# Both MLPs keep their results over the blocks; half of one more block by seven products; adaLN sums and tile pool rearranged

## The chip, the cores and the metric

The kernel runs on one core of a Trainium2 chip. The metric is the device time of one execution in microseconds (us). A run of the kernel before is given as the median of three executions.

## The reference

Two layers over x of 256 tokens by 2048. Each layer does, with a conditioning vector c,

```
mod = silu(c) @ w_ada[l] + b_ada[l]          # 2048 x 12288: six vectors of 2048
sh_a, sc_a, g_a, sh_m, sc_m, g_m = split(mod)
h = rmsnorm(x) * (1 + sc_a) + sh_a
mix = concat(diff_attention(h @ w_in ...), latent_attention(...)) @ w_o[l]
x = x + g_a * mix
h = rmsnorm(x) * (1 + sc_m) + sh_m
y = square(relu(h @ w_mlp_in[l])) @ w_mlp_out[l]     # 2048 -> 8192 -> 2048
x = x + g_m * y
```

and the end is a last rmsnorm with a weight. All numbers are float32.

## The kernel before

Every weight passes the core once, in pieces of 1 MB (128 x 2048), loaded by SyncE's queue (SP) into a pool of five buffers, `raw`. The tensor engine (PE) multiplies in a rounded 32-bit format; to keep float32 accuracy each weight piece is split: ScalarE (ACT) rounds it to `hi` (L154) and VectorE (DVE) takes the rest, `lo` (L157), each in two halves of 128x1024. A product is then three matmuls: hi with both parts of x, lo with the large part (L314, L315, L317).

The adaLN vectors `mod` come from 192 further loads of 1 MB (`ada`), in the same five buffers; on each, DVE does one multiplication with a running sum over 128x2048 (L383). Which place of the program gets how many of them is set by a rate: each piece of weights adds `self.rate` to a credit, and one `ada` is loaded for each whole credit (`more_ada`). Its sum on DVE is issued at the next piece, behind that piece's last split.

x stays on the chip as two halves of 128 tokens (half 0 and half 1), in four chunks c of 512 columns. A result of an output projection (w_o, w_mlp_out) comes chunk by chunk, in four pieces of weights kq each (`rows`), and `updates` does yg = result * gate (L1320), x += yg (L1322), for both halves; where it is the last addition before a norm, ACT squares x besides (L1336). In the last chunk before a norm half 0 is finished before half 1, so that the norm can begin.

An MLP runs in four blocks fb of 2048 hidden columns. For each block the first matmuls (`wides`, L220 and L223) give `hid`; then the rows of w_mlp_out for this block are applied. Columns 0 to 1023 (chunks 0 and 1) can be done "by seven": for a pair of hidden tiles the 2x2 product of blocks is formed with seven products in place of eight (`seven`, L1202 to L1204), which asks DVE for sums of weight blocks (`comb`), more splits, and sums of hid (`sl`, `sh`); at the end `four` adds the seven results up to four tiles (L1238 to L1251). Layer 1 does all its blocks by seven; layer 0 does half of the hidden tiles of block 3 by seven (the other half by `both_by_k`, L1172 to L1178) and blocks 0 to 2 plainly. At the end of each block `updates` adds gate * result to x; in layer 0 block 0's results wait for block 1, since the gate vector is not there yet.

The Tile framework's scheduler sets each engine's order of instructions from priorities and dependences; the order given here is what it wrote.

Of the kernel before, what the change touches and what calls it, by code (L numbers as in the profile page):

```python
# [19 lines left out]
NK = D // P  # L20
# [4 lines left out]
NFB = DFF // D  # L25
# [70 lines left out]


RATE_A0, RATE_V, RATE_K, RATE_M = 1.1, 1.6, 0.6, 0.75
RATE_P = 1.0
RATE_K1, RATE_A1, RATE_C1, RATE_A2, RATE_V1, RATE_O1 = 0.0, 0.8, 0.3, 0.4, 1.2, 0.8  # L100
FILL = "0|1|2|3||||rlm"


class Trunk:
    def __init__(self, ctx, tc, io):
        self.nc, self.tc, self.io = tc.nc, tc, io
        pool = lambda name, bufs, **k: ctx.enter_context(tc.tile_pool(name=name, bufs=bufs, **k))
        self.cp = pool("cp", 1)
        self.wp = pool("wp", 4)
        self.up = pool("up", 40)  # L110
        self.tp = pool("tp", 6)
        self.sp = pool("sp", 8)
        self.pp = pool("pp", 8, space=bass.MemoryType.PSUM)
        self.dp = pool("dp", 1, space=bass.MemoryType.DRAM)
        self.ada_todo, self.ada_here, self.rate, self.credit = [], [], 0.0, 0.0
        self.sums, self.by_act, self.by_dve = [], [], []
        self.bias_out = None
        self.quiet = False
        self.tot = None
        self.n = 0  # L120
# [18 lines left out]
    def weights(self, src, width=2048, order=None):  # L139
        raw = self.raw(src, width)  # L140
        half = width // 2
        out = []
        for i in range(2):
            w, ins = self.part(raw, i, half, order and order[1], order and order[0])
            out.append(w)
        self.more_ada(ins)
        return out

# [739 lines left out]
    def layer(self, l, acc=None):  # L888
        nc, io = self.nc, self.io
# [32 lines left out]
        kk, qn, kn, qr, vm, a, at, v, o = [], [], [], [], [], [], [], [], []  # L922
# [134 lines left out]
        o = self.mo + o  # L1057
        for kq in (2, 3):
            self.rows_by_k(pss, self.weights(io["w_o"][l, 0, kq]), o, kq)
        self.updates(pss, 0, True)  # L1060
        for c in range(1, 4):
            self.updates(self.rows(io["w_o"][l], o, c, c == 3), c, True)

        self.quiet = False
        self.rate = RATE_K1 if l else RATE_K
        h, banks = self.norm_then_by_k(l, 3, 4, io["w_m0"] if l == 0 else io["w_m01"])
        self.rate = RATE_M
        if l:
            for fb in range(NFB):
                self.block_by_seven(1, fb, fb, h, banks, len(banks))  # L1070
                banks = []
        else:
            self.mlp(h, banks)
        self.quiet = False

    def mlp(self, h, banks):

        io = self.io
        late = []
        for fb in range(NFB - 1):  # L1080
# [8 lines left out]
            if fb == 1:  # L1089
                self.gate(0, 5)  # L1090
            for c in range(4):
                pss = self.rows(io["w_m2"][0, fb], hid, c)
                if fb == 0:
                    late += [self.copy(ps, "y") for ps in pss]
                else:
                    if late:
                        pss = [self.added(late.pop(0), ps) for ps in pss]
                    self.updates(pss, c)
        self.block_by_seven(0, NFB - 1, NFB, h, [], NK // 2)

    def block_by_seven(self, l, fb, b, h, banks, plain):

        io = self.io
        hid, steps, sums = [], [], []
        first = NK * fb - (6 if l else 12)
        if l == 0:
            self.rate = RATE_P
# [18 lines left out]
        if l == 0:  # L1126
            self.rate = RATE_M
        elif fb == 0:
            self.gate(1, 5)
        end = fb == NFB - 1  # L1130
        if end and l == 0:
            done = lambda pss, c: self.updates(pss, c, True)
        else:
            done = self.final if end else self.updates
        first, adds, halves = self.four(sums)
        first()
        light = adds + [lambda c=c: done(halves[c], c) for c in range(2)]
        pss = [self.bank("pr") for _ in range(2)]
        for kq in range(4):
            self.rows_by_k(pss, self.weights(io["w_m2"][l, fb, 2, kq]), hid, kq)  # L1140
            if kq < 3 or not plain:
                light.pop(0)()
        done(pss, 2)
        if plain:
            self.both_by_k(b, plain // 2, hid, halves)
            light.pop(0)()
        if end:
            light.pop(0)()
            pss = self.rows(io["w_m2"][l, fb], hid, 3, True)
        else:  # L1150
            pss = [self.bank("pr") for _ in range(2)]
            for kq in range(4):
                self.rows_by_k(pss, self.weights(io["w_m2"][l, fb, 3, kq]), hid, kq)
                if light:
                    light.pop(0)()
        done(pss, 3)

    def both_by_k(self, b, n, xs, halves):

# [68 lines left out]

        return [five, two]

    def four(self, sums):

        add = self.nc.vector.tensor_tensor
        p1, p2, p3, p4, p5, p6, p7 = sums
        c11, c12, c21, c22 = [self.t("y") for _ in range(4)]

        def first():
            self.nc.scalar.activation(c11, p1, AF.Copy)  # L1238
# [384 lines left out]
def _layout(i):  # L1623
# [21 lines left out]
    for l in range(2):  # L1645
# [26 lines left out]
    blocks = [(1, b) for b in range(NFB)] + [(0, NFB - 1)]  # L1672
# [22 lines left out]
```

## Time and profile before

| | us |
|---|---|
| median of 3 runs | 2147.52 (2147.2 to 2147.98) |
| the profiled execution | 2146.1 |
| its span, first to last instruction | 2144.3 |
| mean granted clock of PE | 0.996 |
| PE busy | 2116.9 (99%) |
| DVE busy | 1810.8 (84%) |
| ACT busy | 1212.5 (57%) |

Matmuls overlap: a row's duration of 0.39 us for a 128x512 matmul holds its way through the engine, and the next one starts 0.23 us later. Two starts, not a duration, tell what one costs. The same holds in small on DVE and ACT. In a timeline "[0.96 <-ACT hi L154]" is the idle time of the engine ahead of that instruction and what ended it.

### The profile page before, as it was taken

What the parts mean: (1) busy time and instruction counts of PE and PEld (TensorE: products, weight loads), DVE (VectorE), ACT (ScalarE), POOL (GpSimd) and SP (SyncE); (2) the same over time, 40 slices, a digit from 0 to 9 for tenths busy, and PEclk for the clock granted to TensorE, in tenths of its full rate; (3) what the DMA queues carried; (4) which work ended last, traced back from release to release, by engine and by line L of the source; (5) the groups of instructions that cost most, each with busy time, mean ns of one, the idle gap of its engine ahead of it and who ended that gap; (6) DMA issues with size and microseconds to landing.
All of it is one profiled execution on the core that took longest, in us unless ns stands there. A gap on an engine that the chain in (4) does not pass through costs nothing.

```text
span 2144.3 us, 29298 instructions
## 1 busy us (share of the span) xinstructions
PE 2116.9 (99%) x11239; PEld 1829.4 (85%) x11239; DVE 1810.8 (84%) x2505; ACT 1212.5 (57%) x1847; POOL 6.2 (0%) x18
## 2 busy tenths in 40 slices
PE   7999999999999999999999999999999999999998
PEld 6899887898888888888888898888888888888886
DVE  8889888988788988889987887778977887897897
ACT  6555663565465355346555576547645765664674
POOL 0000000000000000000000000000000000000000
PEclk8999999999999999999999999999999999999999
DMA  9989898799888888886877767875565574564553
GB/s 397 423 343 339 323 355 346 286 332 361 320 326 348 332 337 324 347 330 252 299 253 290 278 224 287 292 267 192 181 237 183 179 247 146 204 230 175 193 191 128
DMA packets 87244, 594.75 MB, mean 277 GB/s; under 512 B 9856, under 2 KB 10304, under 8 KB 20288
## 3 DMA queue, kind: packets, MB, share of 16 engines
q1 hardware_dynamic: 85536, 586.41, 73.7%
q0 software_dynamic: 848, 5.28, 0.6%
q8 instruction: 88, 1.44, 0.3%
q10 hardware_dynamic: 720, 1.19, 0.1%
q14 instruction: 52, 0.43, 0.1%
HBM read 589.66 MB, written 3.18 MB: 276 GB/s over the span
## 4 chain that ended last, share of the span: by engine, by line
PE 93%; DVE 3%; DMA 2%; ACT 2%; issue 1%; ACTq 0%; DVEq 0%; SPq 0%
PE ps L220 20%; PE ps L223 10%; PE pr L314 10%; PE pr L315 10%; PE pr L317 10%; PE pk L263 3%; PE pk L287 3%; PE pp L1203 2%; PE pp L1202 2%; PE pp L1204 2%; PE pv L301 2%; PE pv L299 2%; PE pv L300 2%; PE pk L197 1%; PE pk L201 1%; PE pk L284 1%
## 5 line engine op out<-in xcount | busy, mean ns | idle before, releaser
L154 ACT ACTIVATE hi<-raw 128x1024 fp32r<-128x1024 f32 (+2 forms) x714 | 713.6, 1015 | 549.0 <-PE pr L315 163.9
L157 DVE TENSOR_TENSOR lo<-raw,hi 128x1024 fp32r<-128x1024 f32 (+2 forms) x714 | 821.1, 1170 | 209.6 <-ACT hi L154 98.8
L220 PE MATMUL ps<-h,hi 128*128 128x512 f32 x1952 | 461.9, 390 | 0.0
L383 DVE SCALAR_TENSOR_TENSOR ada<-ada,cond 128x2048 f32<-128x2048 f32 x192 | 438.5, 2286 | 13.3 <-DMA ada<-in_w_ada 12.8
L220 PEld LDWEIGHTS ps<-h,hi 128*128 128x128 f32 x1952 | 362.3, 188 | 74.7 <-DVE sum L1401 1.9
L314 PE MATMUL pr<-hi,hid 128*128 128x512 f32 x704 | 274.0, 389 | 0.0
L315 PE MATMUL pr<-hi,hid 128*128 128x512 f32 x704 | 273.9, 389 | 0.0
L223 PEld LDWEIGHTS ps<-h,lo 128*128 128x128 f32 x1952 | 247.7, 191 | 8.0
L223 PE MATMUL ps<-h,lo 128*128 128x256 f32 x1952 | 250.3, 283 | 0.0
L317 PE MATMUL pr<-lo,hid 128*128 128x512 f32 x704 | 174.5, 389 | 0.0
L317 PEld LDWEIGHTS pr<-lo,hid 128*128 128x128 f32 x704 | 132.2, 188 | 27.4
L315 PEld LDWEIGHTS pr<-hi,hid 128*128 128x128 f32 x704 | 132.2, 188 | 27.4
L314 PEld LDWEIGHTS pr<-hi,hid 128*128 128x128 f32 x704 | 132.2, 188 | 27.3
L1400 ACT ACTIVATE sum<-ps 128x256 f32<-128x256 f32 x110 | 42.0, 382 | 130.5 <-PE ps L223 130.2
L157 DVE TENSOR_TENSOR lo<-comb,hi 128x1024 fp32r<-128x1024 f32 x66 | 80.2, 1221 | 6.3 <-PE ps L223 6.2
L263 PE MATMUL pk<-hf,w 128*128 128x256 f32 x384 | 83.9, 379 | 0.0
L263 PEld LDWEIGHTS pk<-hf,w 128*128 128x128 f32 x384 | 72.7, 190 | 10.0
L154 ACT ACTIVATE hi<-comb 128x1024 fp32r<-128x1024 f32 x66 | 69.2, 1053 | 11.4 <-PE pp L1204 7.6
L197 PE MATMUL pk<-h,hi 128*128 128x256 f32 x256 | 72.3, 285 | 0.2 <-ACT h L718 0.2
L201 PE MATMUL pk<-h,lo 128*128 128x256 f32 x256 | 72.4, 283 | 0.0
L200 PE MATMUL pk<-h,hi 128*128 128x256 f32 x256 | 72.4, 283 | 0.0
L287 PE MATMUL pk<-h,hi 128*128 128x512 f32 x256 | 67.6, 394 | 0.0
(294 smaller groups left out, 3134.4 us busy)
## 6 DMA issues: line engine op xcount, KB each, us to landing
raw<-in_w_m SPq DMA_DIRECT2D x198, 1024.0 KB, 5.6
ada<-in_w_ada SPq DMA_DIRECT2D x192, 1024.0 KB, 6.4
raw<-in_w_ms SPq DMA_DIRECT2D x40, 1024.0 KB, 5.1
raw<-in_w_o SPq DMA_DIRECT2D x32, 1024.0 KB, 5.7
raw<-in_w_m SPq DMA_DIRECT2D x24, 768.0 KB, 5.6
raw<-in_w_dv SPq DMA_DIRECT2D x16, 1024.0 KB, 6.0
raw<-in_w_t SPq DMA_DIRECT2D x12, 1024.0 KB, 6.6
w<-in_w_a SPq DMA_DIRECT2D x24, 384.0 KB, 13.5
```

What stands on the lines that cost most here:

```text
L154: ins = self.nc.scalar.activation(hi, v, AF.Copy)
L157: ins = self.nc.vector.tensor_tensor(lo, v, hi.bitcast(F32), ALU.subtract)
L197: ins = mm(ps, hi, x[0], start=first, stop=False, skip_group_check=shared)
L201: self.last_mac = mm(ps, lo, x[0], start=False, stop=last, skip_group_check=shared)
L220: mm(ps.rearrange("p a b -> p (a b)"), part(w, k, 0), x[2], start=k == 0, stop=False)
L223: mm(ps[:, 0], part(w, k, 1), x[0], start=False, stop=k == nk - 1)
L263: self.nc.tensor.matmul(ps, v, whole[k], start=first, stop=last, skip_group_check=True)
L287: ins = mm(ps, part(j, 0), both, start=False, stop=False, skip_group_check=True)
L314: mm(ps, xh[:, c], part(i, 0), start=kq == 0 and i == 0, stop=False)
L315: mm(ps, xl[:, c], part(i, 0), start=False, stop=False)
L317: self.last_mm = mm(ps, xh[:, c], part(i, 1), start=False, stop=kq == 3 and i == 3)
L383: ins = nc.vector.scalar_tensor_tensor(w, w, 1.0, self.cond, ALU.mult, ALU.mult, accum_out=acc[:, i : i + 1])
```

## The change

1. The results of a block stay in eight tiles (`kept`); `keep` adds each block's result to them (y += result), and gate * y is added to x once, in the last block. In the last block chunk 3 of what the first three blocks left is added to x early, ahead of the last chunk's rows.
2. Layer 0 does half of block 2 by seven too.
3. The tile pool `up` has 48 buffers, not 40; the scratch of GpSimd's DMA rings is made smaller for it.
4. `gate(l, 5)` moves to the last block of each layer.
5. In w_o the `ada` sums that are due stand ahead of `updates`, not behind, for chunks 0 to 2.
6. Rates: in layer 0's half blocks 0.5 in place of 1.0, in layer 1's MLP 0.1 while sevens run and 0.5 in rows, in layer 1's w_o 0.7 in place of 0.8. All `ada` loads stay 192; layer 0's MLP has 72 of them in place of 87, and 16 (all of them for layer 1's last gate) now lie in layer 1's MLP, which had none behind its norm. One more lies within the norm ahead of that MLP.

```
-RATE_P = 1.0
-RATE_K1, RATE_A1, RATE_C1, RATE_A2, RATE_V1, RATE_O1 = 0.0, 0.8, 0.3, 0.4, 1.2, 0.8
+RATE_P = 0.5
+RATE_Q1, RATE_M1 = 0.1, 0.5
+RATE_K1, RATE_A1, RATE_C1, RATE_A2, RATE_V1, RATE_O1 = 0.0, 0.8, 0.3, 0.4, 1.2, 0.7
...
-        self.up = pool("up", 40)
+        self.up = pool("up", 48)
...
-        self.updates(pss, 0, True)
-        for c in range(1, 4):
-            self.updates(self.rows(io["w_o"][l], o, c, c == 3), c, True)
+        for c in range(4):
+            if c:
+                pss = self.rows(io["w_o"][l], o, c, c == 3)
+            if c < 3:
+                self.ada_sums(self.last_lo)
+            self.updates(pss, c, True)
...
             for c in range(4):
-                pss = self.rows(io["w_m2"][0, fb], hid, c)
-                if fb == 0:
-                    late += [self.copy(ps, "y") for ps in pss]
-                else:
-                    if late:
-                        pss = [self.added(late.pop(0), ps) for ps in pss]
-                    self.updates(pss, c)
-        self.block_by_seven(0, NFB - 1, NFB, h, [], NK // 2)
+                self.keep(self.rows(io["w_m2"][0, fb], hid, c), c)
+        for fb in range(2, NFB):
+            self.block_by_seven(0, fb, NFB + fb - 2, h, [], NK // 2)
+
+    def keep(self, pss, c):
+
+        if self.kept[c] is None:
+            self.kept[c] = [self.copy(ps, "y") for ps in pss]
+        else:
+            for y, ps in zip(self.kept[c], pss):
+                self.added(y, ps)
...
+        if end:
+            last = lambda c: self.final(self.kept[c], c) if l else self.updates(self.kept[c], c, True)
+            for c in range(2):
+                light += [lambda c=c: last(c)]
...
-        done(pss, 2)
+        self.keep(pss, 2)
...
         if end:
-            light.pop(0)()
+            self.updates(self.kept[3], 3)
+            for f in light:
+                f()
+            last(2)
             pss = self.rows(io["w_m2"][l, fb], hid, 3, True)
...
-    nc = bacc.Bacc("TRN2", target_bir_lowering=False, num_devices=1)
+    nc = bacc.Bacc("TRN2", target_bir_lowering=False, num_devices=1, dynamic_dma_scratch_size=2048)
```

Line numbers above L1060 rise by 2 and those below by 16, so L157 (the split lo) is L159 afterwards, L383 (ada) is L385, L1320 and L1322 are L1336 and L1338.

Three places of DVE's order. The first is layer 0's w_o at the end of chunk 0: lo is the second half of a weight piece's split, yg and x the update of the two halves, base the sum of squares. Before:

```order
L157 TENSOR_TENSOR lo_3224<-raw_3221,hi_3223 128x1024
L157 TENSOR_TENSOR lo_3228<-raw_3221,hi_3227 128x1024
L1320 TENSOR_TENSOR yg_3209<-pr_3057,bias 128x512
L383 SCALAR_TENSOR_TENSOR ada_3183,macc_84<-ada_3183,cond 128x2048
L1322 TENSOR_TENSOR x<-x,yg_3209 128x512
L1320 TENSOR_TENSOR yg_3214<-pr_3058,bias 128x512
L1322 TENSOR_TENSOR x<-x,yg_3214 128x512
```

and now:

```order
L385 SCALAR_TENSOR_TENSOR ada_3183,macc_84<-ada_3183,cond 128x2048
L399 TENSOR_TENSOR mod_81<-macc_82,vec 128x2
L159 TENSOR_TENSOR lo_3225<-raw_3222,hi_3224 128x1024
L1336 TENSOR_TENSOR yg_3210<-pr_3058,bias 128x512
L159 TENSOR_TENSOR lo_3229<-raw_3222,hi_3228 128x1024
L1338 TENSOR_TENSOR x<-x,yg_3210 128x512
L1336 TENSOR_TENSOR yg_3215<-pr_3059,bias 128x512
L1338 TENSOR_TENSOR x<-x,yg_3215 128x512
```

The ada left its place between yg and x and stands ahead of both splits; one split now lies between yg and x. The same is done one chunk later on DVE, and there ACT's second squaring moves behind one split hi.

The second place is layer 0's last block, from the last plain results (y<-pr) to the last yg of the last rows. Before:

```order
L1322 TENSOR_TENSOR x<-x,yg_9634 128x512
L383 SCALAR_TENSOR_TENSOR ada_9661,macc_96<-ada_9661,cond 128x2048
L1320 TENSOR_TENSOR yg_9639<-y_9303,bias 128x512
L395 SCALAR_TENSOR_TENSOR mod_95<-macc_96,vec 128x2
L157 TENSOR_TENSOR lo_9731<-raw_9728,hi_9730 128x1024
L1322 TENSOR_TENSOR x<-x,yg_9639 128x512
L157 TENSOR_TENSOR lo_9735<-raw_9728,hi_9734 128x1024
L1320 TENSOR_TENSOR yg_9644<-y_9305,bias 128x512
L157 TENSOR_TENSOR lo_9741<-raw_9738,hi_9740 128x1024
L1322 TENSOR_TENSOR x<-x,yg_9644 128x512
L157 TENSOR_TENSOR lo_9745<-raw_9738,hi_9744 128x1024
```

and now, from the split that answers to lo_9741 on:

```order
L159 TENSOR_TENSOR lo_9755<-raw_9752,hi_9754 128x1024
L1336 TENSOR_TENSOR yg_9649<-y_5017,bias 128x512
L159 TENSOR_TENSOR lo_9759<-raw_9752,hi_9758 128x1024
L1338 TENSOR_TENSOR x<-x,yg_9649 128x512
L1336 TENSOR_TENSOR yg_9654<-y_5168,bias 128x512
L1338 TENSOR_TENSOR x<-x,yg_9654 128x512
L1360 TENSOR_TENSOR base_9636<-xsq_9635 128x2
L159 TENSOR_TENSOR lo_9823<-raw_9820,hi_9822 128x768
L1336 TENSOR_TENSOR yg_9659<-y_5170,bias 128x512
L159 TENSOR_TENSOR lo_9827<-raw_9820,hi_9826 128x768
L1338 TENSOR_TENSOR x<-x,yg_9659 128x512
L1336 TENSOR_TENSOR yg_9810<-pr_9664,bias 128x512
```

In the row before, the last split (lo_9745) is followed by the sums of squares alone and then by yg of half 0 of the last rows. Now two updates of kept results (five instructions of 128x512) and the norm's two splits stand between the last split (lo_9759) and that yg (yg_9810).

The third place is layer 1's block 0, near the end of its sevens, on DVE: comb are sums of weight blocks, lo<-comb their splits, sum the joining of `wides`. Before:

```order
L1211 TENSOR_TENSOR comb_14055<-raw_14053 128x1024
L157 TENSOR_TENSOR lo_13971<-comb_13949,hi_13970 128x1024
L1194 TENSOR_TENSOR sl_13898<-comb_13892,sh_13897 128x512
L1401 SCALAR_TENSOR_TENSOR sum_13901<-ps_13902,sum_13901 128x256
L157 TENSOR_TENSOR lo_13984<-raw_13981,hi_13983 128x1024
L157 TENSOR_TENSOR lo_13988<-raw_13981,hi_13987 128x1024
L157 TENSOR_TENSOR lo_14026<-comb_13949,hi_14025 128x1024
L1212 TENSOR_TENSOR comb_14055<-raw_14053,comb_14055 128x512
```

and now:

```order
L1227 TENSOR_TENSOR comb_14073<-raw_14071 128x1024
L1210 TENSOR_TENSOR sl_13912<-comb_13906,sh_13911 128x512
L1417 SCALAR_TENSOR_TENSOR sum_13915<-ps_13916,sum_13915 128x256
L159 TENSOR_TENSOR lo_13987<-comb_13965,hi_13986 128x1024
L159 TENSOR_TENSOR lo_14000<-raw_13997,hi_13999 128x1024
L159 TENSOR_TENSOR lo_14004<-raw_13997,hi_14003 128x1024
L385 SCALAR_TENSOR_TENSOR ada_13927,macc_98<-ada_13927,cond 128x2048
L159 TENSOR_TENSOR lo_14044<-comb_13965,hi_14043 128x1024
L399 TENSOR_TENSOR mod_97<-macc_98,vec 128x2
L1228 TENSOR_TENSOR comb_14073<-raw_14071,comb_14073 128x512
```

An ada and its mod have come in between the splits; from there to the last two splits of comb both kernels have the same instructions in nearly the same order.

## Rows read from the trace of the kernel before

**Rows 1.** The page's first part: busy time, share of the span, instructions.

```profile
PE 2116.9 (99%) x11239; PEld 1829.4 (85%) x11239; DVE 1810.8 (84%) x2505; ACT 1212.5 (57%) x1847; POOL 6.2 (0%) x18
```

**Rows 2.** The page's chain of work that ended last, by engine.

```profile
PE 93%; DVE 3%; DMA 2%; ACT 2%; issue 1%; ACTq 0%; DVEq 0%; SPq 0%
```

**Rows 3.** PE's waits: what for, us in total, times, longest us.

```profile
PE pr L314 <- ACT hi L154: 2.7, 3, 1.0
PE pp L1203 <- DVE lo L157: 0.7, 4, 0.2
PE pp L1202 <- ACT sh L1193: 0.7, 3, 0.3
```

**Rows 4.** Timeline, PE, layer 0's w_o: start us, us, instruction, idle time before.

```profile
348.25 1.98 PE L317 MATMUL pr<-lo,do 128*128 128x512 f32 x8
350.06 0.39 PE L314 MATMUL pr<-hi,mo 128*128 128x512 f32 x1
...
356.62 0.50 PE L314 MATMUL pr<-hi,mo 128*128 128x512 f32 x1 [0.96 <-ACT hi L154]
...
368.58 0.50 PE L314 MATMUL pr<-hi,do 128*128 128x512 f32 x1 [0.79 <-ACT hi L154]
...
380.78 0.50 PE L314 MATMUL pr<-hi,mo 128*128 128x512 f32 x1 [0.99 <-ACT hi L154]
```

**Rows 5.** Timeline, DVE, layer 0's w_o, end of chunk 0.

```profile
350.04 0.69 DVE L1320 TENSOR_TENSOR yg<-pr,bias 128x512 f32<-128x512 f32 x1 [2.96 <-PE pr L317]
350.64 2.28 DVE L383 SCALAR_TENSOR_TENSOR ada<-ada,cond 128x2048 f32<-128x2048 f32 x1
...
352.85 0.69 DVE L1322 TENSOR_TENSOR x<-x,yg 128x512 f32<-128x512 f32 x1
```

**Rows 6.** Timeline, ACT, layer 0's w_o.

```profile
353.57 0.63 ACT L1336 ACTIVATE sq<-x 128x512 f32<-128x512 f32 x1 [8.12 <-DVE x L1322]
...
355.53 1.99 ACT L154 ACTIVATE hi<-raw 128x1024 fp32r<-128x1024 f32 x2
...
367.48 2.01 ACT L154 ACTIVATE hi<-raw 128x1024 fp32r<-128x1024 f32 x2 [7.23 <-DMA raw<-in_w_o]
...
379.05 0.63 ACT L1336 ACTIVATE sq<-x 128x512 f32<-128x512 f32 x1 [2.75 <-DVE x L1322]
```

**Rows 7.** Timeline, SP, layer 0's w_o: a load's issue.

```profile
361.20 0.33 SPq L173 DMA_DIRECT2D raw<-in_w_o  x1
```

**Rows 8.** Timeline, DVE, layer 0's last block and the norm behind it.

```profile
1083.09 1.37 DVE L1178 TENSOR_TENSOR y<-pr,y 128x512 f32<-128x512 f32 x2 [1.31 <-PE pr L1174]
...
1098.34 1.23 DVE L157 TENSOR_TENSOR lo<-raw,hi 128x1024 fp32r<-128x1024 f32 x1
...
1101.45 0.69 DVE L1320 TENSOR_TENSOR yg<-pr,bias 128x512 f32<-128x512 f32 x1 [1.41 <-PE pr L317]
...
1116.36 2.29 DVE L383 SCALAR_TENSOR_TENSOR ada<-ada,cond 128x2048 f32<-128x2048 f32 x1
```

**Rows 9.** Timeline, PE, the same stretch.

```profile
1100.34 1.07 PE L317 MATMUL pr<-lo,hid 128*128 128x512 f32 x4
...
1111.25 0.62 PE L284 MATMUL pk<-h,lo 128*128 128x256 f32 x3 [0.24 <-ACT h L718]
```

**Rows 10.** Windows of layer 1's block 0: length, busy PE, PEld, DVE, ACT, POOL, PEclk, DMA share, GB/s.

```profile
1540.00:1550.00 10.00, 10.00 (x53) 8.62 (x52) 10.00 (x13) 5.56 (x7) 0.00 (x0) 1.00 0.39 120
```

**Rows 11.** Timeline, DVE, the last splits of the sevens of layer 1's block 0.

```profile
1556.05 2.36 DVE L157 TENSOR_TENSOR lo<-comb,hi 128x1024 fp32r<-128x1024 f32 x2
1558.32 2.36 DVE L157 TENSOR_TENSOR lo<-raw,hi 128x1024 fp32r<-128x1024 f32 x2
```

**Rows 12.** Timeline, PE, the same place.

```profile
1557.33 0.50 PE L1203 MATMUL pp<-lo,sh 128*128 128x512 f32 x1
1557.67 0.40 PE L1204 MATMUL pp<-hi,sl 128*128 128x512 f32 x1
```

**Rows 13.** Timeline, DVE, the last rows of layer 1.

```profile
2130.58 0.69 DVE L1320 TENSOR_TENSOR yg<-pr,bias 128x512 f32<-128x512 f32 x1 [2.23 <-PE pr L317]
```

More of the change, by code (lines that the diff above doesn't have):

```diff
@@ L145, in weights @@
             out.append(w)
+        self.last_lo = ins
         self.more_ada(ins)
@@ L1067, in layer @@
         self.rate = RATE_M
+        self.kept = [None] * 4
         if l:
@@ L1078, in mlp @@
         io = self.io
-        late = []
-        for fb in range(NFB - 1):
+        for fb in range(2):
             hid = []
@@ L1088, in mlp @@
                 hid += self.relu2(self.joined(ps, self.t("sum")))
-            if fb == 1:
-                self.gate(0, 5)
             for c in range(4):
-                pss = self.rows(io["w_m2"][0, fb], hid, c)
-                if fb == 0:
-                    late += [self.copy(ps, "y") for ps in pss]
-                else:
-                    if late:
-                        pss = [self.added(late.pop(0), ps) for ps in pss]
-                    self.updates(pss, c)
-        self.block_by_seven(0, NFB - 1, NFB, h, [], NK // 2)
+                self.keep(self.rows(io["w_m2"][0, fb], hid, c), c)
[7 more added lines that the diff above has]
+                self.added(y, ps)
     def block_by_seven(self, l, fb, b, h, banks, plain):
@@ L1105, in block_by_seven @@
         first = NK * fb - (6 if l else 12)
-        if l == 0:
-            self.rate = RATE_P
+        start, end = self.kept[0] is None, fb == NFB - 1
+        self.rate = RATE_Q1 if l else RATE_P
         for m in range(0, plain, 2):
@@ L1125, in block_by_seven @@
             f()
[L1126 to L1132, printed above, removed]
-        else:
[L1134 to L1137, printed above, removed]
+        self.rate = RATE_M1 if l else RATE_M
+        if end:
+            self.gate(l, 5)
+        first, adds, halves = self.four(sums, self.u if start else self.t)
+        first()
+        if start:
+            light = adds
+            self.kept[:2] = halves
+        else:
+            light = adds + [lambda c=c: self.keep(halves[c], c) for c in range(2)]
+        if end:
+            last = lambda c: self.final(self.kept[c], c) if l else self.updates(self.kept[c], c, True)
+            for c in range(2):
+                light += [lambda c=c: last(c)]
         pss = [self.bank("pr") for _ in range(2)]
@@ L1140, in block_by_seven @@
             self.rows_by_k(pss, self.weights(io["w_m2"][l, fb, 2, kq]), hid, kq)
-            if kq < 3 or not plain:
+            if light and (kq < 3 or not plain):
                 light.pop(0)()
-        done(pss, 2)
+        self.keep(pss, 2)
         if plain:
             self.both_by_k(b, plain // 2, hid, halves)
-            light.pop(0)()
+            if light:
+                light.pop(0)()
         if end:
-            light.pop(0)()
+            self.updates(self.kept[3], 3)
+            for f in light:
+                f()
+            last(2)
             pss = self.rows(io["w_m2"][l, fb], hid, 3, True)
[L1150 to L1156, printed above, removed]
+            if l:
+                self.final(pss, 3)
+            else:
+                self.updates(pss, 3, True)
+            return
+        pss = [self.bank("pr") for _ in range(2)]
+        for kq in range(4):
+            self.rows_by_k(pss, self.weights(io["w_m2"][l, fb, 3, kq]), hid, kq)
+            if light:
+                light.pop(0)()
+        self.keep(pss, 3)
     def both_by_k(self, b, n, xs, halves):
@@ L1229, in seven, with four @@
         return [five, two]
-    def four(self, sums):
+    def four(self, sums, room):
         add = self.nc.vector.tensor_tensor
         p1, p2, p3, p4, p5, p6, p7 = sums
-        c11, c12, c21, c22 = [self.t("y") for _ in range(4)]
+        c11, c12, c21, c22 = [room("y") for _ in range(4)]
         def first():
@@ L1671, in _layout @@
         keep["w_m2"].append(np.stack([_kcols(f["w_mlp_out"][l][D * b : D * b + D]) for b in range(NFB)]))
-    blocks = [(1, b) for b in range(NFB)] + [(0, NFB - 1)]
+    blocks = [(1, b) for b in range(NFB)] + [(0, b) for b in range(2, NFB)]
     a["w_ms"] = np.stack([_kblocks(f["w_mlp_out"][l][D * b : D * b + D, :1024]) for l, b in blocks])
```

## Prediction

> **What bounds the kernel.** I read the page's busy shares first, then the chain that ended last, then PE's waits, and only then stretches. PE is busy for 99% of the span [rows 1] and 93% of the chain is PE [rows 2], so time can go only where PE executes fewer matmuls or waits less. What a matmul costs is the distance of two starts: eight of 128x512 take from 348.25 to 350.06, 1.81 us or 0.227 each [rows 4]. Apart from the start of the kernel and the norms, PE waits in two kinds of places: three times for ACT's `hi` in layer 0's w_o, 2.7 us in all, and at ends of sevens for DVE's `lo` and ACT's `sh`, 0.7 us each [rows 3]. DVE is busy for 84% on average [rows 1], but in places without any gap: from 1540 to 1550 in layer 1's block 0 its 10.00 us are full [rows 10]. So I price each edit of DVE's order by whether the stretch has idle time. Prices: an update or `keep` of 128x512 takes 0.60 us (350.04 to 350.64), an `ada` 2.21 us (350.64 to 352.85) [rows 5], a split 1.14 us (1556.05 to 1558.32 for two) [rows 11].
>
> **1. Matmuls.** Half of block 2 has 8 hidden tiles. Plainly, chunks 0 and 1 take 8 x 2 chunks x 2 halves x 3 = 96 matmuls of 128x512; by seven 4 pairs x 7 x 3 = 84. Twelve fewer at 0.227: -2.7 us. PE is the bound there before and after, so I count it in full.
>
> **2. DVE and ACT work in total.** Combining sums and splits for four more pairs cost DVE about 22 us: four more splits net at 1.14, 16 operations of 128x512 at 0.60, 16 small ones at an estimated 0.20, four 128x1024 sums at 1.14. The kept results take 32 operations of 128x512 away in balance, 19 us. DVE's total stays where it is; what counts is where the work lies. Layer 0's block 2 gets an end of sevens of its own. At all ends of sevens together PE waits seven times, 1.4 us in all [rows 3], so two waits of 0.2 at one end: +0.4, bounds 0 and 1.
>
> **3. Layer 0's w_o.** The three waits of PE end at 356.62, 368.58 and 380.78, with 0.96, 0.79 and 0.99 shown [rows 4]; by starts against 0.227 they are 1.1, 0.95 and 1.15, or 3.2 in all. The first: yg begins at 350.04 after 2.96 us of idle, the `ada` runs from 350.64 to 352.85 ahead of x [rows 5], ACT idles 8.12 us for that x, squares, and starts `hi` at 355.53 [rows 6], with 1 us to run; PE wants it at 355.66 (356.62 less 0.96). Now the `ada` runs in the idle 2.96 us, with one split (1.14) between yg and x: x starts 1.07 us earlier, so `hi` is in time; -1.0. The second: `hi` at 367.48 waited for a load issued at 361.20 [rows 6, 7], 6.28 us before. The load is issued when a buffer comes free by the `ada` ahead of it, which runs about 1.1 us earlier; but PE also arrives 1.0 earlier, so nearly all of it stays: -0.1. The third: ACT's square at 379.05 waits 2.75 us for x [rows 6], with `hi` behind it. Now that `hi` stands ahead of the second square; a later yg behind its `ada` can keep some 0.3 of the 1.15, which leaves -0.9. Sum -2.0; bounds -3.2 (all three go) and 0 (loads are late throughout, below).
>
> The Trainium skill ("DMA: Bandwidth & Descriptors", section "Anatomy of one DMA — SWDGE (gpsimd) path") fits one DMA at about 2.0 us plus the bytes over 436 GB/s. For 1 MB that would be an estimated 4.4 us, and the second wait would go too, -0.85 more. The row shows 6.28 us with other loads under way, so I keep the row.
>
> **4. Layer 0's last block.** DVE is full behind 1083.09, where it starts the last plain results after 1.31 us idle, until its last split from 1098.34; then it idles 1.41 until yg at 1101.45 [rows 8]. In the new order there are, from the first result to the end of the last split, 15 operations at 0.60, six splits at 1.14 and one `ada`: 9.0 + 6.8 + 2.2 = 18.0, so it ends at 1101.1 in place of 1099.5. PE uses this split in the second half of the group that starts at 1100.34 [rows 9], at 1100.8: PE waits 0.4. Behind it stand five updates and the norm's two 768-wide splits (about 0.87 each by their width), so yg of half 0 runs near 1106 in place of 1101.45, and x of half 1 about 0.6 later than before. The norm's first matmul at 1111.25 [rows 9] hangs on that x: with the squares behind it some 0.75 us later altogether. The order ahead of 1083.09 has two more operations of 128x512 for 1.31 of idle, which just fits; I take +1.1, bounds 0 and +3.
>
> **5. Layer 1's MLP.** Of the 16 `ada` that now lie here, 12 lie in stretches of rows, where DVE has no updates any more (three of four blocks lost them); these cost nothing. Four lie in stretches of sevens. Block 0 has one: from its place to the last splits of `comb` both orders hold the same work, and DVE has no gap there [rows 10]. The first of these splits starts at 1556.05, is done by 1557.19 [rows 11], and PE uses it at 1557.33, where 0.34 to the next row at 1557.67 in place of 0.23 already shows a wait of 0.1 [rows 12]. 2.21 us and a small `mod` less 0.14 of room: +2.1, bounds 0 (PE's own order has other matmuls to give in between) and 2.3. The other three stand in blocks 1 and 2, where I see idle time of DVE between pairs; with one end of sevens that is ordered better, I take -0.4, bounds -1 and +4.4 (two `ada` in full). The one `ada` in the norm ahead of the MLP costs nothing: the first layer-1 norm has one at the same place, at 1116.36 [rows 8], and no wait of PE names it [rows 3].
>
> **6. The end.** In the last rows eight more operations (4.8 us) meet DVE's idle 2.23 before 2130.58 [rows 13] and some slack of the splits: +0.2, bounds 0 and +1.
>
> **7. At nothing.** Pool size, ring scratch and the gates' move: the gate's coefficients are wanted a dozen us after they are issued, GpSimd is busy 6.2 us in the whole span [rows 1]. If the gate came late, the first yg in the last blocks would wait, with splits behind it on DVE; I hold 0 to +1.
>
> Sum: -2.7 + 0.4 - 2.0 + 1.1 + 2.1 - 0.4 + 0.2 = -1.3 us on the profiled 2146.1, or 2144.8. The median of the runs is 1.4 above that execution, so the forecast is 2146.2: no change that a measurement can tell. (About 0.2% or 4.3 us is what it can.)
>
> **Rivals.**
> (a) DVE's extra work never reaches PE. PE's order changes with DVE's, so between a late split and its use other matmuls may stand. For it: the waits at ends of sevens are only tenths [rows 3], though DVE is full there [rows 10]. Against it: those tenths show that it has no reserve [rows 12]. Then -2.7 - 3.2 - 0.4 + 0.4 = -5.9, or 2141.6: faster.
> (b) The w_o waits stay, since the loads set them: the second wait's `hi` came straight from a load [rows 6]. Earlier instructions then only wait longer. Against it: in the first wait ACT waited for x [rows 6]. Then 2.0 above the forecast, 2148.2: no change.
> (c) Slower: the `ada` in layer 1's sevens take their full price. The mechanism is the one that I count for block 0, in all four places: 4 x 2.28 = 9.1 in place of 2.1 - 0.4, so +7.4, and 2153.6. Three of them uncovered give +5.1 and 2151.3, so it decides (2151.8) when three of the four are uncovered and half a microsecond is lost elsewhere. For it: 10.00 of 10 [rows 10]. Against it: DVE's mean of 84% [rows 1] leaves gaps between the pairs.
>
> **How the numbers follow.** Forecast 0.47, own range 2144 to 2149; (a) 0.25; (b) 0.17; (c) 0.11. The range of eight in ten reaches to (a) and to where (c) begins: 2141.5 to 2151.5. Faster by over 0.2% needs under 2143.2: most of (a) and a little of the forecast's lower edge, 0.26. Slower needs over 2151.8: (c), 0.11. The rest, 0.63, is no change.
>
> **What would show it.** In the changed kernel's waits of PE: L314 for `hi` once, near 0.8 us, in place of three times; a wait of some 2 us of L1203 for `lo` at the end of block 0's sevens in layer 1; a wait below 1 us for a split in layer 0's last rows, and the norm's first matmul there later behind the last row than now. If no wait of 2 us stands in layer 1, (a) is right; if several do, (c). If L314 still waits three times, for loads, it is (b). A new wait at a place that I priced at nothing, for the gate's row above all, makes it wrong.

## The result, and the profile after

The changed kernel takes 2150.65 us (median of 22 runs, 2147.11 to 2153.48) against 2147.24 us (22 runs, 2145.38 to 2149.92) for the kernel before: ratio 1.0015 [1.0009, 1.0021], so it is 3.4 us slower, where 1.3 less was forecast. The profiled execution took 2151.39 us with a span of 2149.6. PE has the twelve matmuls less that were counted, DVE and ACT have the same shares as before [rows 1], and the share of PE in the chain of waits fell from 93% [rows 2] to 88%, that of DVE rose from 3% to 7%. The page's first part and its chain, after:

```profile
PE 2119.2 (99%) x11227; PEld 1829.0 (85%) x11227; DVE 1814.9 (84%) x2520; ACT 1228.6 (57%) x1864; POOL 6.2 (0%) x18
PE 88%; DVE 7%; DMA 2%; ACT 2%; issue 1%; ACTq 0%; DVEq 0%; SPq 0%
```

PE's waits of the changed kernel (what for, us in total, times, longest us), which answer to [rows 3]; the waits of the head and those of a few tenths are left out:

```profile
PE pn L1375 <- DVE rms L1371: 2.7, 1, 2.7
PE pp L1219 <- DVE lo L159: 2.2, 2, 1.5
PE pp L1218 <- ACT hi L156: 0.9, 1, 0.9
...
PE pr L316 <- ACT hi L156: 0.5, 1, 0.5
```

L316, which was L314, waits once in place of three times. L1219 (L1203) and L1218 (L1202) have waits of 1.5 and 0.9 where they had tenths; the rest of L1219's 2.2 is a wait of 0.65 at 1748 us. The first row is new: L1375 is `pn<-ident,rms`, the matmul that spreads the norm's reciprocal root, and it waits 2.7 us.

To see where the time went, I cut each profile at events that all kernels have and took the differences of their times from the timelines: attention 0's first `pn<-ones,acc`, the first turning (transposition, `tx`) of x in each norm, the first `pk` of the stage behind it, and the end of the last PE instruction.

```
                 attn 0+w_o   MLP 0   norm behind it   attn 1   MLP 1   tail
before             250.26    704.91        4.55        329.33   690.85   8.34
after              249.34    702.78        8.98        329.35   693.14   8.69
```

The stretches that the change touches give, in order: w_o -2.0 (this is read from PE's starts ahead of its first wait to those at its end, since the stretch ahead of w_o varies by over 1 us between profiles of unchanged code), MLP 0 -2.1, norm +4.4, MLP 1 +2.3, tail +0.35. That is +3.0 together; the other 0.4 of the medians' 3.4 I don't place. One stretch is far from its forecast: the norm behind layer 0's MLP.

PE in that norm, after (timeline: start, us, instruction, idle time before):

```profile
1104.87 0.60 PE L1387 MATMUL tx<-ident,x 128*128 128x128 f32 x4
1108.20 0.46 PE L1375 MATMUL pn<-ident,rms 128*128 128x128 f32 x2 [2.73 <-DVE rms L1371]
1108.50 4.01 PE L1387 MATMUL tx<-ident,x 128*128 128x128 f32 x20
1112.35 0.39 PE L1375 MATMUL pn<-ident,rms 128*128 128x128 f32 x2
1112.57 1.04 PE L1387 MATMUL tx<-ident,x 128*128 128x128 f32 x8
1113.85 0.62 PE L286 MATMUL pk<-h,lo 128*128 128x256 f32 x3 [0.24 <-ACT h L720]
```

and the same three steps before:

```profile
1106.70 0.60 PE L1371 MATMUL tx<-ident,x 128*128 128x128 f32 x4
1107.13 0.39 PE L1359 MATMUL pn<-ident,rms 128*128 128x128 f32 x2
1107.36 2.35 PE L1371 MATMUL tx<-ident,x 128*128 128x128 f32 x20
```

PE makes the first four turnings (columns 0 to 255 of x, both halves), then stands 2.73 us at the spread of half 0's reciprocal. The 20 turnings behind it read columns 256 to 1535, whose last update starts at 1104.29 on DVE and takes 0.68, so they need nothing that is late; but the kernel orders them behind the spread (`turned(1, self.last_spread, ...)`), and PE runs them there. An order with the spread behind these turnings was not run. When they run they take 4.01 us in place of 2.35. The stretch is 4.43 longer; 2.73 + 1.66 = 4.39 of it are these two.

What the spread waits for, on DVE, after:

```profile
1098.20 1.21 DVE L159 TENSOR_TENSOR lo<-raw,hi 128x1024 fp32r<-128x1024 f32 x1
...
1104.89 0.68 DVE L1336 TENSOR_TENSOR yg<-pr,bias 128x512 f32<-128x512 f32 x1
...
1105.90 0.69 DVE L1338 TENSOR_TENSOR x<-x,yg 128x512 f32<-128x512 f32 x1
...
1107.90 0.16 DVE L1371 RECIPROCAL rms<-rms 128x1 f32<-128x1 f32 x1
```

and on ACT between them (squares of x, and the root):

```profile
1106.67 0.63 ACT L1352 ACTIVATE sq<-x 128x512 f32<-128x512 f32 x1 [0.41 <-DVE base L1362]
...
1107.43 0.29 ACT L1366 ACTIVATE rms<-xsq,base 128x1 f32<-128x1 f32 x1
```

The last split of the rows ends at 1099.3. Then DVE runs five instructions of 128x512 that add kept results to x and the norm's two splits, and only at 1104.89 yg of half 0; from there x, the square, the root and the reciprocal follow, 3.2 us to the reciprocal's end. The reciprocal now stands behind half 1's update too, but the root ends at 1107.72, so this order costs at most 0.2 of it. Before, that yg ran at 1101.45 [rows 8], and the reciprocal was done 1.45 us ahead of PE's spread at 1107.13:

```profile
1105.52 0.16 DVE L1355 RECIPROCAL rms<-rms 128x1 f32<-128x1 f32 x1
```

The granted clock in this stretch, after (windows: length, busy PE, PEld, DVE, ACT, POOL, PEclk, DMA share, GB/s):

```profile
1106.00:1108.00 2.00, 0.00 (x0) 0.00 (x0) 1.97 (x5) 1.29 (x4) 0.45 (x1) 1.00 0.87 344
1108.00:1110.00 2.00, 1.80 (x10) 1.83 (x11) 0.67 (x3) 1.02 (x3) 0.08 (x1) 0.67 0.64 134
1110.00:1112.00 2.00, 2.00 (x11) 2.00 (x11) 0.84 (x3) 0.65 (x2) 0.00 (x0) 0.50 0.94 397
1112.00:1114.00 2.00, 1.76 (x15) 1.52 (x14) 1.04 (x3) 1.26 (x3) 0.00 (x0) 0.97 0.00 0
```

PE had been idle for the wait; then the clock stands at 0.50, the level of 1.2 GHz, in most of the four microseconds in which the 20 turnings run, and near 1.00 (2.4 GHz) behind them. In these windows one turning starts 0.21 us behind the other, where it was 0.11 in the kernel before, which accounts for the longer turnings.

### The profile page after: what moved, and what is told of

It reads as the page before. It is cut to its first block, busy times and chain, and to the rows that moved or that the text cites. A ratio compares the mean times of both kernels' runs of the same rounds, so it can differ in the third digit from the quotient of the medians.

```text
span 2149.6 us, 29311 instructions
## 1 busy us (share of the span) xinstructions
PE 2119.2 (99%) x11227; PEld 1829.0 (85%) x11227; DVE 1814.9 (84%) x2520; ACT 1228.6 (57%) x1864; POOL 6.2 (0%) x18
## 4 chain that ended last, share of the span: by engine, by line
PE 88%; DVE 7%; DMA 2%; ACT 2%; issue 1%; ACTq 0%; DVEq 0%; SPq 0%
PE ps L222 19%; PE ps L225 10%; PE pr L319 9%; PE pr L316 9%; PE pr L317 9%; DVE lo L159 3%; PE pk L265 3%; PE pk L289 3%; PE pp L1219 2%; PE pp L1220 2%; PE pp L1218 2%; PE pv L303 2%; PE pv L301 2%; PE pv L302 2%; PE pk L199 1%; PE pk L203 1%
## 5 line engine op out<-in xcount | busy, mean ns | idle before, releaser
L159 DVE TENSOR_TENSOR lo<-raw,hi 128x1024 fp32r<-128x1024 f32 (+2 forms) x714 | 817.1, 1164 | 215.6 <-ACT hi L156 92.8
L385 DVE SCALAR_TENSOR_TENSOR ada<-ada,cond 128x2048 f32<-128x2048 f32 x192 | 437.8, 2283 | 13.1 <-DMA ada<-in_w_ada 12.4
L316 PE MATMUL pr<-hi,hid 128*128 128x512 f32 x640 | 249.1, 389 | 0.0
L317 PE MATMUL pr<-hi,hid 128*128 128x512 f32 x640 | 249.0, 389 | 0.0
L319 PE MATMUL pr<-lo,hid 128*128 128x512 f32 x640 | 159.1, 389 | 0.0
L319 PEld LDWEIGHTS pr<-lo,hid 128*128 128x128 f32 x640 | 120.1, 188 | 25.2 <-DVE lo L159 0.3
L316 PEld LDWEIGHTS pr<-hi,hid 128*128 128x128 f32 x640 | 120.2, 188 | 25.0
L317 PEld LDWEIGHTS pr<-hi,hid 128*128 128x128 f32 x640 | 120.2, 188 | 25.0
L159 DVE TENSOR_TENSOR lo<-comb,hi 128x1024 fp32r<-128x1024 f32 x74 | 89.8, 1218 | 5.2 <-PE ps L225 4.9
L156 ACT ACTIVATE hi<-comb 128x1024 fp32r<-128x1024 f32 x74 | 77.8, 1054 | 16.1 <-PE pp L1220 9.7
```

Of the source, the lines that this page charges most:

```text
L156: ins = self.nc.scalar.activation(hi, v, AF.Copy)
L159: ins = self.nc.vector.tensor_tensor(lo, v, hi.bitcast(F32), ALU.subtract)
L316: mm(ps, xh[:, c], part(i, 0), start=kq == 0 and i == 0, stop=False)
L317: mm(ps, xl[:, c], part(i, 0), start=False, stop=False)
L319: self.last_mm = mm(ps, xh[:, c], part(i, 1), start=False, stop=kq == 3 and i == 3)
L385: ins = nc.vector.scalar_tensor_tensor(w, w, 1.0, self.cond, ALU.mult, ALU.mult, accum_out=acc[:, i : i + 1])
```

## The experiments

The theory: DVE's work in layer 0's last rows, the kept updates with one `ada` among them, makes half 0's reciprocal late, and costs the wait and then the clock; layer 1's block 0 pays for its `ada` as forecast. The rival: the loss lies in the other edits (w_o's moved sums, block 2's half by seven), or in the new pools and gates. Runs of one comparison shared a chip with the kernel before, whose median was 2146.85 to 2147.46 in them. "Less than the changed kernel" compares medians of two comparisons; taking each from its own kernel before alters these differences by up to 0.4 us. The intervals reach about 0.09% to either side, 1.9 us; e8 alone is a single run. Lengths of stretches are from one profile each.

**e1: the kernel before, with only the sums of `ada` in w_o moved.**

```
+            if c < 3:
+                self.ada_sums(self.last_lo)
             self.updates(pss, c, True)
```

> The kernel before with the move of the ada sums in w_o alone. My theory (PE's waits there came from x standing behind an ada on DVE, and ACT's hi behind the squares of x): PE waits once for hi in layer 0's w_o, near 0.7 us, in place of three times, and the time is 2.1 us below the kernel before (2145.1 for 2147.2). Rival (the loads set these waits): three waits as before, 2.7 us in PE's view of waits, and no change. Rival 2 (the changed kernel's new order of the two engines there costs more later): the waits go but the time stays within 0.5 us.

2145.67 us against 2147.46, ratio 0.9996 [0.9987, 1.0004]. One wait of PE's three at these places is left:

```profile
368.51 0.50 PE L315 MATMUL pr<-hi,do 128*128 128x512 f32 x1 [0.44 <-ACT hi L155]
```

By the starts of PE around the three places it gains 1.1, 0.0 and 1.0 us; the median's -1.8 agrees, but its interval doesn't exclude zero. w_o's edit is no loss.

**e2: the changed kernel, with no `ada` in layer 1's sevens** (they go to the rows instead).

```
-RATE_Q1, RATE_M1 = 0.1, 0.5
+RATE_Q1, RATE_M1 = 0.0, 0.6
```

> The changed kernel with no ada in layer 1's stretches of sevens (rate 0.0 in place of 0.1), and 0.6 in place of 0.5 in its rows, so that the same 16 are done there. My theory (one ada of 2.2 us at the end of block 0's sevens, where DVE has no gap, is what PE waits for): PE's waits of 1.5 us for lo and 0.9 us for hi in that place go, 2.2 to 2.5 us below the changed kernel. Rival (the waits come from the different order of comb and sums there, not from the ada): waits of over 1.5 us stay at that place and the time falls by less than 0.8. Rival 2: the denser ada in the rows push splits late there and give it back.

2146.40 us, ratio 0.9999 [0.9990, 1.0008]: 4.25 less than the changed kernel. MLP 1 takes 690.49 in place of 693.14, and the waits of 1.5 and 0.9 are gone; that is 2.65. In this profile another 1.67 is in the norm, which this edit doesn't touch: the wait is the same, but the turnings take their old time. PE there:

```profile
1106.93 0.46 PE L1375 MATMUL pn<-ident,rms 128*128 128x128 f32 x2 [2.73 <-DVE rms L1371]
1107.23 2.35 PE L1387 MATMUL tx<-ident,x 128*128 128x128 f32 x20
```

and its windows over the wait and behind it:

```profile
1105.00:1107.00 2.00, 0.07 (x1) 0.10 (x1) 1.75 (x5) 1.28 (x5) 0.53 (x1) 1.00 0.75 308
1107.00:1109.00 2.00, 2.00 (x19) 2.00 (x20) 1.02 (x3) 1.36 (x4) 0.00 (x0) 1.00 0.65 201
```

Here the clock stayed at 1.00. So the wait of 2.73 costs 2.76 by itself (a stretch of 7.31 against 4.55), and the fall of the clock, which may or may not follow it, 1.67 more.

**e3: the changed kernel, with no `ada` in layer 0's last chunk of rows.**

```
             last(2)
+            if l == 0:
+                self.rate = 0.0
```

> The changed kernel with rate 0 in the last rows of layer 0's MLP, so that one ada sum less stands between that block's last results and the norm; later places take it. My theory (DVE is behind by about its added updates there, so the norm's first reciprocal is late, PE stands for 2.7 us, its clock falls to half and 20 transpositions take 4.0 us in place of 2.35): with 2.2 us less on DVE the wait for the reciprocal is under 0.8 us, the clock stays at 1.00, and that stretch (first transposition to the norm's first matmul) takes 4.5 to 5.5 us in place of 9.0: 3.5 to 4.5 us below the changed kernel. Rival (the order of the reciprocal behind half 1's update decides, whatever DVE's load): the wait stays over 1.5 us and the time falls by less than 1.5. Rival 2 (ACT's squares are the late ones): the same.

2147.53 us, ratio 1.0001 [0.9992, 1.0009]: 3.1 less than the changed kernel, where 3.5 to 4.5 were expected. The norm is back at 4.55 with no wait. But the one `ada` that left shifts all that follow: layer 1's attention has 30 of them at other places, where the changed kernel has 31, and layer 1's MLP 18 in place of 16. The attention is 2.2 longer, with one new wait of PE:

```profile
1270.86 0.50 PE L302 MATMUL pv<-lo,h 128*128 128x512 f32 x1 [1.59 <-DVE lo L159]
```

MLP 1 takes 691.68, 1.5 less than in the changed kernel: the `ada` in block 0's sevens stand earlier there, and the waits of 1.5 and 0.9 at their end are gone. What an `ada` costs hangs on its place.

**e4: both edits.**

> Both mends of the changed kernel in one (no ada in layer 1's sevens, none in layer 0's last rows). If the two places are independent and hold what was lost: 5.7 to 6.9 us below the changed kernel, near 2144.3, and 2.5 to 3.5 us below the kernel before. Rival (what is taken from these places stands in the way elsewhere, in layer 1's rows or its attention): less than 4 us, no better than the kernel before.

2146.44 us, ratio 0.9995 [0.9986, 1.0004]: 4.2 less than the changed kernel, where 5.7 to 6.9 were expected. Norm 4.55 and MLP 1 690.26, but attention 1 takes 333.06, 3.7 more. The wait at L302 is e3's, with the `ada` at nearly the same shifted places; but here the clock falls behind it (PE's timeline, then a window):

```profile
1269.21 0.50 PE L302 MATMUL pv<-lo,h 128*128 128x512 f32 x1 [1.59 <-DVE lo L159]
1270.00:1272.00 2.00, 2.00 (x6) 1.57 (x5) 2.00 (x3) 1.35 (x2) 0.00 (x0) 0.50 0.91 258
```

In e3 it stayed at 1.00 there. So 2.2 of the 3.7 come of the shifted `ada`, and 1.5 of the clock.

**e5: as e4, with `ada` shifted forward** into layer 0's blocks 0 and 1, so that attention keeps its places. The first edit stands at the start of layer 0's MLP, the second behind the sevens of a block (`end` is the last block), the third behind layer 0's MLP; e4's two stay.

```
+        self.rate = 0.82
-        self.rate = RATE_M1 if l else RATE_M
+        self.rate = RATE_M1 if l else (0.5 if end else RATE_M)
...
+            self.credit = 0.4
```

> The changed kernel with no ada in layer 1's sevens, and with two ada sums fewer in layer 0's last rows; these two are done earlier, in layer 0's plain blocks, so that layer 1's attention gets the same ada at the same places as the changed kernel has. My theory (the two places cost 2.4 and 2.8 us or more, and the run with both mends lost the gain only because its ada moved within layer 1's attention, where a wait of 1.6 us for lo appeared): no wait for the reciprocal, the stretch from the norm's first transposition to its first product 4.5 us, layer 1's attention 239.7 us long as in the kernel before, and 2142.5 to 2144 in all, 3.5 to 5 us below the kernel before. Rival (DVE has no room for two more sums in the plain blocks either): layer 0's MLP gets longer by 2 us or more and the time is no better than the kernel before.

2145.59 us against 2146.85, ratio 0.9996 [0.9987, 1.0004]. Attention 1 is at 329.33 and the norm at 4.55, but MLP 0 takes 704.51, 1.7 more than in the changed kernel: PE's starts slip by 0.7 up to 583 us, in the blocks where the `ada` went, without a wait of PE that the profile names; of the rest, 0.3 lies from 1001 to 1051 us and the remainder in pieces of 0.1 to 0.2. The total misses the 2142.5 to 2144 expected. An `ada` is a load as well as a sum: in blocks 0 and 1 (402 to 755 us) ACT waits for loads of weights twice as long as in the changed kernel, whose row is the first here:

```profile
ACT hi L156 <- DMA raw<-in_w_m: 29.8, 10, 4.3
ACT hi L156 <- DMA raw<-in_w_m: 64.2, 21, 7.3
```

That the loads set the 1.7 is not shown by a run of its own.

**e6: the changed kernel with PE's wait filled**: 24 turnings of x into a bank that nobody reads, between the norm's first four turnings and the spread.

```
+        if l and sh == 0:
+            dump = self.bank("dump")
+            for i in range(24):
+                ins = nc.tensor.transpose(dump[:, i // 2 % 2, i % 2 * P : i % 2 * P + P], self.xr[:, 0, :P], self.ident)
+                self.behind(ins, self.last_turned)
+            self.last_turned = ins
```

> The changed kernel with 24 needless transpositions (their result is read by nobody) in PE's order ahead of the norm's first product with the reciprocal, where PE stood for 2.7 us. My theory (part of what that wait costs is PE's clock, which the profile showed at half for the next 3 us, in that run): the wait shrinks to under 0.3 us, the clock stays at 1.00 behind it and the 20 transpositions take 2.35 us; the stretch takes 7.3 us, and the time is 0 to 1.7 us below the changed kernel, by how often the clock falls there. Rival (the transpositions are slow because x or the banks are late, not the clock): they take 4 us again.

2148.70 us, ratio 1.0009 [1.0000, 1.0019], 1.95 less than the changed kernel; the two intervals overlap, so the time alone doesn't show a gain. The reciprocal starts 3.03 us behind the first turning, as in the changed kernel, but the 20 turnings take their old time:

```profile
1104.34 2.78 PE L760 MATMUL dump<-ident,x 128*128 128x128 f32 x24
1107.14 0.49 PE L1381 MATMUL pn<-ident,rms 128*128 128x128 f32 x2
1107.46 2.35 PE L1393 MATMUL tx<-ident,x 128*128 128x128 f32 x20
```

The stretch is 7.25, as in e2. So two parts are told apart: a wait of some 2.7, and 1.7 of clock. That the filling kept the clock up is not shown by this one profile, since in e2 the clock stayed up with the wait unfilled.

The same profile shows the fall at another place. In layer 1's block 0, behind waits that the changed kernel has there too, its clock falls (PE's timeline, then windows):

```profile
1556.12 0.50 PE L1225 MATMUL pp<-lo,hid 128*128 128x512 f32 x1 [1.55 <-DVE lo L159]
1558.48 0.60 PE L1224 MATMUL pp<-hi,sh 128*128 128x512 f32 x1 [0.94 <-ACT hi L156]
1558.00:1560.00 2.00, 1.52 (x4) 1.24 (x5) 2.00 (x3) 1.38 (x2) 0.00 (x0) 0.69 0.47 61
1560.00:1562.00 2.00, 2.00 (x6) 1.54 (x6) 1.81 (x2) 0.70 (x1) 0.00 (x0) 0.50 0.83 340
```

Matmuls of 128x512 start 0.43 us apart there, not 0.23, and PE is 1.6 us behind the changed kernel after it. MLP 1 takes 694.38.

**e7: e5 with block 2 wholly plain** (`range(3)` and `range(3, NFB)` in place of 2), which undoes the half by seven.

```
-        for fb in range(2):
+        for fb in range(3):
...
-        for fb in range(2, NFB):
+        for fb in range(3, NFB):
```

> The kernel labelled e5_same_attention with layer 0's block 2 plain again. My theory (twelve matmuls at 0.227 us, less a wait of 0.5 us at the added end of sevens): layer 0's MLP, from its norm's first transposition to the next norm's, is 2.0 to 2.4 us longer than in e5. Rival (PE gains nothing by the seven products, since their splits hold it up): the same length within 0.5 us.

2147.13 us, ratio 1.0005 [0.9996, 1.0014], against e5's 2145.59; MLP 0 takes 706.15 against 704.51, 1.64 more, where 2.0 to 2.4 were expected. The half by seven isn't alone in this: block 2 now runs at the rate of the plain blocks, and 86 `ada` lie in layer 0's MLP against 73 in e5 (3 against 16 in layer 1's).

**e8: the changed kernel without the gate's product** in the additions of chunks 0 to 2 of layer 0's last block (the result is added to x as it is, so six operations of 128x512 go, 3.6 us at 0.60); that part of the computation is left out, the `ada` stays.

```
-            last = lambda c: self.final(self.kept[c], c) if l else self.updates(self.kept[c], c, True)
+            last = lambda c: self.final(self.kept[c], c) if l else self.ungated(self.kept[c], c)
```

> The changed kernel with the last addition of chunks 0 to 2 in layer 0's MLP without the gate's product (left out): six operations of 128x512 fewer on DVE, 3.6 us, in the last rows; the ada stays where it was. My theory (any 2 us less of DVE's work there would do, it need not be the ada): the wait for the reciprocal goes and the stretch from the norm's first transposition to its first product takes 4.5 us. Rival (it was the ada that was in the way, by its length or its load): a wait of over 1.5 us stays.

2145.82 us in one run. The norm takes 4.56, with no wait at the spread. (MLP 1 takes 694.24: the clock falls to 0.51 behind block 0's waits, as in e6.) So it is not the `ada` as such: 3.6 us less of other work of DVE ahead of half 0's reciprocal take the wait away too.

**e9: the two `ada` put into the plain halves** of blocks 2 and 3, where e5 had them in blocks 0 and 1. The last edit is e3's.

```
-RATE_P = 0.5
-RATE_Q1, RATE_M1 = 0.1, 0.5
+RATE_P = 0.75
+RATE_Q1, RATE_M1 = 0.0, 0.6
...
+            self.credit = 0.4
-        self.rate = RATE_M1 if l else RATE_M
+        self.rate = RATE_M1 if l else (0.5 if end else RATE_M)
+            if l == 0:
+                self.rate = 0.0
```

> As the kernel labelled e5_same_attention (no ada in layer 1's sevens, two ada fewer in layer 0's last rows), but these two are done in the plain halves of layer 0's blocks 2 and 3 (rate 0.75 there in place of 0.5), not in blocks 0 and 1. My theory: the two sums cost nothing there, so layer 0's MLP takes 702.8 us as in the changed kernel (e5: 704.5), its norm 4.55, layer 1's attention 329.3 and its MLP 690.5: 2143.0 to 2145 in all and 2.5 to 4 us below the kernel before. Rival (wherever the two sums go in layer 0's MLP they cost 1.7 us, since loads or DVE are full there): 704.5 again, and the time of e5.

2143.37 us (11 runs, 2141.28 to 2144.69) against 2147.12, ratio 0.9983 [0.9974, 0.9991]: faster than both kernels. MLP 0 702.76, norm 4.56, attention 1 329.36, MLP 1 690.72: no stretch pays for another here. Since the moved sums in w_o, the half by seven, the pool and the gates are all in this kernel, the loss of the changed kernel didn't lie in them. PE at the norm no longer waits:

```profile
1104.74 0.60 PE L1390 MATMUL tx<-ident,x 128*128 128x128 f32 x4
1105.18 0.39 PE L1378 MATMUL pn<-ident,rms 128*128 128x128 f32 x2
1105.40 2.35 PE L1390 MATMUL tx<-ident,x 128*128 128x128 f32 x20
```

since DVE has half 0's yg 4.15 us earlier than in the changed kernel (the norm's first turnings start within 0.13 us of each other in the two), and its reciprocal ends 0.4 us ahead of PE's spread:

```profile
1100.74 0.68 DVE L1339 TENSOR_TENSOR yg<-pr,bias 128x512 f32<-128x512 f32 x1
...
1104.63 0.16 DVE L1374 RECIPROCAL rms<-rms 128x1 f32<-128x1 f32 x1 [0.24 <-ACT rms L1369]
```

**e10: the changed kernel once more**, for a second profile.

> The changed kernel once more, unchanged. If PE's clock falls in most executions behind the 2.7 us wait: the 20 transpositions take 4.0 us again, and the time is near 2150.6. If it was that one profile: 2.35 us, the stretch 7.3 us, and a time near 2148.5 to 2149. The stretches ahead of layer 0's w_o, which the change leaves alone, will differ between profiles by up to 1.5 us either way.

2150.47 us, ratio 1.0016 [1.0007, 1.0025]. Wait and clock are there again, norm 8.83, MLP 1 692.82:

```profile
1106.64 0.77 PE L1375 MATMUL pn<-ident,rms 128*128 128x128 f32 x2 [2.73 <-DVE rms L1371]
1107.20 3.60 PE L1387 MATMUL tx<-ident,x 128*128 128x128 f32 x20
```

## Why the prediction was wrong, step by step

The direction was wrong: a gain of 1.3 was forecast, a loss of 3.4 came, which lies inside the range given (2141.5 to 2151.5) but beyond the forecast's own (2144 to 2149).

**Steps 1 and 2, matmuls and the new end of sevens: right.** -2.3 was forecast (-2.7 + 0.4). MLP 0 is 2.13 shorter in the changed kernel and 2.15 in e9. Counted over PE's starts, it has the twelve matmuls less (2.72) and 0.60 more of gaps; 0.65 come from 852 to 902 us, where the new end of sevens lies, and the rest evens out. The pair of e7 and e5 (1.64) has 13 `ada` moved with it and is no measure.

**Step 3, w_o: right.** -2.0 was forecast, -1.0, -0.1 and -0.9 at the three places; -1.1, +0.1 and -0.95 came, and e1 alone gives the same pattern. The second wait, which a load sets, stayed, as its row had it: the load was issued at 362.35 and `hi` began 5.98 us later. By the Trainium skill's fit ("DMA: Bandwidth & Descriptors", section "Anatomy of one DMA — SWDGE (gpsimd) path") it would have gone for an estimated 0.85 more; but that fit is for DMAs issued by GpSimd, and these loads are issued by SyncE among others, so this wait neither confirms nor refutes it:

```profile
369.44 0.50 PE L316 MATMUL pr<-hi,do 128*128 128x512 f32 x1 [0.50 <-ACT hi L156]
```

**Step 4, layer 0's last block: this failed.** +1.1 was forecast with bounds of 0 and +3, and +4.43 came (+4.28 in e10; +2.76 in e2, where the clock stayed up). The first half of the step nearly holds: DVE's work from the first plain result to the end of the last split was put at 18.0 us and took 18.1 (1081.20 to 1099.34). The wait of 0.4 for that split isn't in PE's waits. What failed is the sentence "The norm's first matmul at 1111.25 [rows 9] hangs on that x": I followed x of half 1 to the end of the norm, and asked of nothing in between. PE has an instruction for half 0 ahead of it, the spread, with 20 turnings behind that. My own "yg of half 0 runs near 1106" was enough: the chain from yg to the reciprocal's end is 3.2 us in the trace after, so it would be done near 1109.2, against a spread at 1107.13, a row of before that the prediction doesn't use. That gives 2 us of wait. The rest comes of DVE, which needs 23.7 us from the first plain result to yg where my terms add up to 22.8, 0.53 of it idle for ACT's `hi`. That PE comes earlier by steps 1 to 3 adds nothing: its results start DVE's stretch, which begins 1.89 us earlier, and PE's first turning 1.83. The clock, 1.5 to 1.7 more for the stretch in two of three profiles, I had not thought of at all.

**Step 5, layer 1's MLP: right in sum, and by its mechanism.** +2.1 was forecast for block 0's `ada`, and a wait of some 2 us of L1203. PE after, at that place:

```profile
1558.80 0.50 PE L1219 MATMUL pp<-lo,hid 128*128 128x512 f32 x1 [1.53 <-DVE lo L159]
...
1561.16 0.50 PE L1218 MATMUL pp<-hi,sh 128*128 128x512 f32 x1 [0.93 <-ACT hi L156]
```

2.46 in two pieces, and e2, which has no `ada` there, has neither. Of the three others one can be seen: the wait of 0.65 at 1748 us, which e2 doesn't have either, with 0.2 us between the two kernels around it. MLP 1 grew by 2.29 and in e10 by 1.97, where +1.7 was forecast with -0.4 for the others. That it came so close is in part luck: in e6 and e8, with the same `ada` and the same waits, the clock fell behind them and MLP 1 grew by 3.5 and 3.4.

**Steps 6 and 7: right.** The tail is 0.35 longer for +0.2. No wait names a gate or the pool.

**The rivals.** (a) fell with the waits at L1219 and at the spread; (b) with two of three waits gone in w_o; (c) had the right sign, by the wrong place: of four `ada` in layer 1's sevens one costs what it says, and the other loss is a layer earlier. The measured sum of the touched stretches is +3.0 against -1.3, and 3.3 of these 4.3 are step 4. What remains unsettled is what sets e5's 1.7 in MLP 0, and what decides whether the clock falls behind a wait.

## What to carry to other kernels

When an engine's work gets later, follow it to the first instruction in the waiting engine's queue that needs it, not to the last: everything that stands behind that one waits too, whether it needs the result or not. Before the change, half 0's reciprocal had 1.45 us of reserve at that meeting: that is the number to hold against a delay of several microseconds on DVE. Work that may run anywhere (here the `ada`) has no fixed price. One in a stretch where DVE has no gap cost PE 2.5 us; two in blocks 0 and 1 came with 1.7; with two in the plain halves of blocks 2 and 3 and none in the sevens of layer 1, the same change is 0.17% faster than the kernel before, in place of 0.15% slower. Idle time of DVE alone doesn't tell these places apart; idle time of the loads may. In the changed kernel DVE is busy for 76% of the time from 560 to 600 us, in block 1, and for 80% from 800 to 845, in block 2; the DMA share is 0.80 and 0.45 there.

A change of rate moves every later `ada`: e3 and e7 show that an edit of one place is not an edit of that place alone.

## What the runs showed of the hardware

A wait of 2.7 us on PE was followed by a granted clock of 0.50 to 0.67 in two profiles of the changed kernel, and the 20 turnings took 4.01 and 3.60 us; after a wait of the same length in e2 it stayed at 1.00 and they took 2.35. With PE kept busy by 24 turnings of no use (e6) it stayed at 1.00 at that place. Windows of e10, where the fall comes with the wait:

```profile
1105.00:1107.00 2.00, 0.36 (x2) 0.39 (x3) 1.46 (x5) 1.56 (x5) 0.53 (x1) 0.84 0.65 271
1107.00:1109.00 2.00, 2.00 (x11) 2.00 (x11) 0.70 (x2) 0.47 (x3) 0.00 (x0) 0.50 0.76 221
```

So one wait has two prices, 2.8 and 4.3 to 4.4 us, and the page's busy share shows neither: PE reads 99% in the kernel before and in the one after.

The norm is not the only such place. From 45 us to the last matmul, the twelve profiles have nine waits of PE of 1.5 us or more: at the norm (the changed kernel, e2, e10), in layer 1's block 0 (the changed kernel, e6, e8, e10) and in layer 1's attention (e3, e4). Behind five of them the clock falls below 0.97 in a window of 2 us (the changed kernel and e10 at the norm, e6 and e8 in block 0, e4 in the attention), and nowhere else. Each fall cost 1.5 to 1.7 us. Whether it falls differs between executions of the same code, so a stretch of one profile can't be compared with that of another before the clock in both is read.
